# Two heads side by side in the values products, dilated scores in head pairs, and a hint ahead of the overflow branch

## The chip, the cores and the metric

The kernel runs on one core of a Trainium2 chip, in one launch. The time is device microseconds of one execution; the number to be told is the median of several runs. The engines are TensorE (PE in the profile; PEld are its weight loads), VectorE (DVE), ScalarE (ACT), GpSimd (POOL) and SyncE (SP, which issues most DMAs).

## The reference

Two blocks of two layers each work on 256 tokens of width 1024, all in fp32. A layer of the first block has a mixer of global attention (8 query heads, 2 key heads) and dilated attention (12 heads in three groups of 4, summed by their log-sum-exp weights), and then 16 experts with two chosen per token. A layer of the second block has four branches, among them neighbourhood attention and attention on a memory (4 heads each), and a feed-forward net. Cut to the attention, which the change touches:

```python
def _global_gqa(q, k, v):                       # 8 heads of 64
    sc = jnp.einsum('bqgrd,bkgd->bgrqk', qi, k).astype(jnp.float32) * scale
    p = jax.nn.softmax(sc, axis=-1)
    return jnp.einsum('bgrqk,bkgd->bqgrd', p.astype(v.dtype), v)

def _dilated_group(q, k, v, window, dilation, slopes):   # three groups of 4 heads
    sc = jnp.einsum('bqhd,bqkhd->bhqk', qi, kg).astype(jnp.float32) * scale + bias[None, :, None, :]
    sc = jnp.where(valid[None, None], sc, -jnp.inf)
    lse = jax.nn.logsumexp(sc, axis=-1)
    p = jnp.exp(sc - lse[..., None])
    o = jnp.einsum('bhqk,bqkhd->bqhd', p.astype(v.dtype), vg)
    return o, lse.transpose(0, 2, 1)
# in _mixer: the three groups of one head are one softmax over all their keys
    wts = jax.nn.softmax(jnp.stack(lses, 0), axis=0)
    out_b = jnp.sum(wts[..., None].astype(h.dtype) * jnp.stack(outs, 0), 0).reshape(b, s, B_OUT)

def memory_attention(q, mk, mv):                # neighbourhood attention is alike, with a bias
    sc = jnp.einsum('bhsd,bhmd->bhsm', q, mk).astype(jnp.float32) * (q.shape[-1] ** -0.5)
    p = jax.nn.softmax(sc, axis=-1)
    return jnp.einsum('bhsm,bhmd->bhsd', p.astype(mv.dtype), mv)
```

## The kernel before

Weights come in blocks of 128x2048 fp32 through SP's queue into four buffers (`wraw`). Each block is split into a high part by ScalarE (`whi`, L60) and a low part by VectorE (`wlo`, L66), and a product with weights is three matmuls of such parts (`mm3`, L251 to L253). Attention itself works in plain fp32.

Tokens lie in two tiles of 128. `scores` and `exps` (L376, L379) take the maximum on VectorE and the exponent on ScalarE, which also sums it into `zz`. `values` then transposes the probabilities on PE (L1045, in `full_attn` L1545), ScalarE copies them out of PSUM into `pt`, and PE multiplies with the probabilities as the stationary operand and 64 columns of values as the moving one (L1052, L1551): tokens come out on the partitions. After all heads `heads_out` (L386, L391) multiplies by the reciprocal of the sums and transposes back, and `split_to` (L398, L399) makes a high and a low part for the next product.

The dilated attention goes over 4 heads and 2 token tiles. Each step makes three scores products of 256 columns, one for each of the three groups (L1088), with 64 rows of the array since a head has 64 features, adds the bias on VectorE (L1089), and after the exponent has 6 transposes (L1100), two copies (L1102) and 6 values products (L1107).

Between these steps stand jobs that need only PE and weights: `fill` takes one from a list (projections and gates, 48 matmuls of 256 columns each), `tick` takes a piece of the conditioning (`ada_acc`, L456, on VectorE). The instructions of GpSimd and SP stand as written; those of PE, VectorE and ScalarE are ordered by the Tile scheduler, except where the program turns that off (`manual_schedule`).

In the experts `moe` reads a flag after the fourth: if a group has over 128 tokens, `moe_rest` (fp32 products for the rest) runs, else it is jumped over (L1330). With the tokens of this case it is jumped over in both layers. On PE `moe_rest` is 4 groups of 80 matmuls and transposes: 16 to gather, 2 transposes, 2 for the weights, 4 experts of 14, and 4 to scatter.

Of the kernel before, what the change touches and what calls it, by code (L numbers as in the profile page):

```python
# [8 lines left out]
F = mybir.dt.float32  # L9
# [3 lines left out]
OP = mybir.AluOpType  # L13
AX = mybir.AxisListType

DEPTH = 2
# [7 lines left out]
SLOPES = [2.0 ** (-8.0 * (h + 1) / 12) for h in range(12)]  # L24
TU = ((0, 2, 3, 6), (2, 3, 4, 6))
# [10 lines left out]
NB8, NRAW, NHL, NT2, NZ1 = 9, 4, 6, 6, 4  # L36
# [136 lines left out]
class Net:  # L173
# [205 lines left out]
            nc.scalar.activation(p[:, i], s[:, i], AF.Exp, bias=nm[:, i:i + 1], accum_out=zz[i])  # L379
        return p  # L380

    def heads_out(self, o, rz, nh, t, hi, lo):

        nc = self.nc
        n = self.t2([128, nh, 64], name="on")
        nc.vector.tensor_mul(n, o.rearrange("p (h d) -> p h d", d=64), rz[:, :, None].to_broadcast([128, nh, 64]))  # L386
        nf = n.rearrange("p h d -> p (h d)")
        p = self.tp()
        m = nh // 2
        for f in range(m):  # L390
            nc.tensor.transpose(p[:, f * 128:(f + 1) * 128], nf[:, f * 128:(f + 1) * 128], self.ident)  # L391
        ts = slice(t * 128, (t + 1) * 128)
        self.split_to(hi[:, :, ts], lo[:, :, ts], p[:, :m * 128].rearrange("p (f w) -> p f w", f=m))

    def split_to(self, hi, lo, ps, scale=None):
        nc = self.nc
# [543 lines left out]
    def mixer(self, l, hT):  # L940
        nc, a = self.nc, self.a
        w = a["win"][l]
# [69 lines left out]
        for jj in range(2):  # L1012
            p = self.tp()
# [12 lines left out]
        ob = [self.acc("oacc") for _ in range(2)]  # L1026

        def scores(j):
            pr = []
# [8 lines left out]
            return pr  # L1038

        def values(j, pr):  # L1040
            for h in range(2):
                p = self.tp()
                for t in range(2):
                    for c in range(2):
                        nc.tensor.transpose(p[:, c * 256 + t * 128:c * 256 + (t + 1) * 128],  # L1045
                                            pr[h][:, t, c * 128:(c + 1) * 128], self.ident)
                pt = self.t2([128, 2, 256], name="pt")
                nc.scalar.copy(pt, p.rearrange("p (c q) -> p c q", c=2))
                n = 2 * j + h
                for t in range(2):  # L1050
                    for c in range(2):
                        nc.tensor.matmul(ob[t][:, n * 64:(n + 1) * 64], pt[:, c, t * 128:(t + 1) * 128],  # L1052
                                         va[:, c, h * 64:(h + 1) * 64], start=(c == 0), stop=(c == 1))
        self.bg_on = True
        for j in range(4):
            pr = scores(j)
# [4 lines left out]
                self.tick()  # L1061
            self.fill()
            values(j, pr)
        rz = self.small([128, 2, 8], "att_rz", 2)
        nc.vector.reciprocal(rz, zz)
        for t in range(2):
            self.heads_out(ob[t], rz[:, t], 8, t, oa[:, 0], oa[:, 1])
        if l == DEPTH - 1:
            self.decay_log(0)

# [6 lines left out]
        od = [self.acc("obacc") for _ in range(2)]  # L1077
        for j in range(4):
            hs = slice(j % 2 * 64, (j % 2 + 1) * 64)
            for t in range(2):  # L1080
                sb = self.sm.tile([128, 3, 256], F, name="sbias", tag="z1", bufs=NZ1)
                s = self.sb()
                for g in range(3):
                    if g == 2:
                        s = self.sb()
                    sv = s[:, (g % 2) * 256:(g % 2 + 1) * 256]
                    ch = 2 * g + j // 2
                    nc.tensor.matmul(sv, qdT[hs, ch, t * 128:(t + 1) * 128], kdT[hs, ch, :], start=True, stop=True)  # L1088
                    nc.vector.scalar_tensor_tensor(sb[:, g], dist[t][g], -SLOPES[4 * g + j], sv,  # L1089
                                                   op0=OP.mult, op1=OP.add)  # L1090
                self.exps(sb.rearrange("p g w -> p (g w)")[:, None, :], [zz[:, t, j:j + 1]], 1, 768, True)
                if (2 * j + t) in TU[l]:
                    self.tick()
                self.fill()
                pt = self.sm.tile([128, 3, 256], F, name="ptd", tag="z1", bufs=NZ1)
                for g0, n in ((0, 2), (2, 1)):
                    p = self.tp()
                    for g in range(g0, g0 + n):
                        for c in range(2):
                            nc.tensor.transpose(p[:, (2 * (g - g0) + c) * 128:(2 * (g - g0) + c + 1) * 128],  # L1100
                                                sb[:, g, c * 128:(c + 1) * 128], self.ident)
                    nc.scalar.copy(pt[:, g0:g0 + n], p[:, :n * 256].rearrange("p (g w) -> p g w", g=n))  # L1102
                for g in range(3):
                    h = 4 * g + j
                    for c in range(2):
                        v = vd0[:, c, h * 64:(h + 1) * 64] if h < 8 else vd1[:, c, (h - 8) * 64:(h - 7) * 64]
                        nc.tensor.matmul(od[t][:, j * 64:(j + 1) * 64], pt[:, g, c * 128:(c + 1) * 128], v,  # L1107
                                         start=(g == 0 and c == 0), stop=(g == 2 and c == 1))
        rz = self.small([128, 2, 8], "att_rz", 2)
        nc.vector.reciprocal(rz[:, :, :4], zz[:, :, :4])  # L1110
        for t in range(2):
            self.heads_out(od[t][:, :256], rz[:, t, :4], 4, t, ob[:, 0], ob[:, 1])
        mr = self.b8([128, 8, 256], name="mr")
        for b in range(2):
            hl = self.wblk(a["wa"][l, b], 4)
# [164 lines left out]
    def moe(self, l, st, sc2, sh2, g2):  # L1280
# [21 lines left out]
        for e in range(NE + 1):  # L1302
# [36 lines left out]
    def moe_y(self, y, g2):  # L1339

        yy = self.b8([128, 2, 1024], R, name="yy")
        vs = []
        for hf in range(2):
            hs = slice(hf * 512, (hf + 1) * 512)
            v = self.t2([128, 512], name="yg")
            self.nc.vector.tensor_mul(v, y[hf], g2[:, hs])
            vs.append(v)
        for hf in range(2):
            hs = slice(hf * 512, (hf + 1) * 512)
            self.split_to(yy[:, 0, hs], yy[:, 1, hs], vs[hf])  # L1350
        return yy

    def moe_rest(self, l, pos, z, sc2, sh2, cw, xb, g2):

# [164 lines left out]
    def full_attn(self, qT, kT, v, voff, bias, oh, ol):  # L1519
# [4 lines left out]
        for hp in range(2):  # L1524
            pr = []
            for i in range(2):
# [11 lines left out]
                pr.append(self.exps(sv, [zz[:, t, h:h + 1] for t in range(2)], inplace=bias is not None))  # L1538
            self.fill()
            for i in range(2):  # L1540
                h = 2 * hp + i
                p = self.tp()
                for t in range(2):
                    for c in range(2):
                        nc.tensor.transpose(p[:, c * 256 + t * 128:c * 256 + (t + 1) * 128],  # L1545
                                            pr[i][:, t, c * 128:(c + 1) * 128], self.ident)
                pt = self.t2([128, 2, 256], name="pt")
                nc.scalar.copy(pt, p.rearrange("p (c q) -> p c q", c=2))  # L1548
                for t in range(2):
                    for c in range(2):  # L1550
                        nc.tensor.matmul(o[:, t * 256 + h * 64:t * 256 + (h + 1) * 64],  # L1551
                                         pt[:, c, t * 128:(t + 1) * 128], v[:, c, voff + h * 64:voff + (h + 1) * 64],
                                         start=(c == 0), stop=(c == 1))
        rz = self.small([128, 2, 8], "att_rz", 2)
        nc.vector.reciprocal(rz[:, :, :4], zz[:, :, :4])
        for t in range(2):
            self.heads_out(o[:, t * 256:(t + 1) * 256], rz[:, t, :4], 4, t, oh, ol)

    def block2(self, l):
        nc, a = self.nc, self.a  # L1560
# [369 lines left out]
```

## Time and profile before

| what | value |
|---|---|
| median of 3 runs | 1786.83 us (1784.20 to 1789.61) |
| profiled execution | 1785.33 us, span 1783.5 us |
| PE busy | 1705.8 us (96%) |
| VectorE busy | 1203.2 us (67%) |
| ScalarE busy | 890.8 us (50%) |
| GpSimd busy | 152.2 us (9%) |
| mean granted clock of PE | 0.974 |
| moved by DMA | 374.16 MB |

The span goes from the first to the last instruction of the program on the chip; some 2 us of the execution lie around it. Busy times of PE are of overlapping matmuls, so that a matmul's price is the distance to the start of the next one. An fp32 matmul is two rows in the trace, one made of `mm3` parts is one row. First-layer attention lies at 80 to 234 us, second-layer at 524 to 682, the experts at 290 to 490 and 740 to 935, the attention of the second block at 1048 to 1094 and 1476 to 1522.

### The profile page before, as it was taken

Reading aid. Unit: us, or ns where it says so; the run is one execution under the profiler, and the core shown is the slowest. Engines: PE = TensorE matmul, PEld = TensorE weight load, DVE = VectorE, ACT = ScalarE, POOL = GpSimd, SP = SyncE. Lnnn points to the kernel's source line nnn. Section 1 sums busy time; section 2 is a strip of 40 time slices with the busy share of each in tenths; the row PEclk is TensorE's granted clock in tenths of the full one; section 3 lists DMA queues with packets and bytes.
Section 4 is the critical chain, followed back from the end, with each engine's and each line's share of the span. In section 5 each row is a group of like instructions: output and inputs, shape, how many; then the busy total and the mean of one; then the engine's idle time right before and its main releaser. Section 6 shows DMA issues by size and latency. Waiting matters only on the chain. (4 is left out here: it accounts for less than half of the span.)

```text
span 1783.5 us, 26246 instructions
## 1 busy us (share of the span) xinstructions
PE 1705.8 (96%) x10666; PEld 1502.2 (84%) x10666; DVE 1203.2 (67%) x1565; ACT 890.8 (50%) x1268; POOL 152.2 (9%) x187
## 2 busy tenths in 40 slices
PE   6899999879999999998999999999999999999999
PEld 6798897768788889776777899999987889989997
DVE  7868778859987746886997465665545555575553
ACT  1544446747654344675765354454444445454442
POOL 3100011110020001101011210000001020000000
PEclk9889999989999999988999999999999999999999
DMA  8768752869757735277976353455555453445552
GB/s 317 273 242 320 255 193 71 301 249 349 274 200 262 269 138 196 76 271 289 337 283 229 124 193 133 172 178 189 185 193 194 165 194 132 164 148 195 183 186 71
DMA packets 56338, 374.16 MB, mean 210 GB/s; under 512 B 6896, under 2 KB 7056, under 8 KB 14224
## 3 DMA queue, kind: packets, MB, share of 16 engines
q1 hardware_dynamic: 50256, 352.41, 55.4%
q0 software_dynamic: 5952, 19.97, 3.2%
q8 instruction: 88, 1.44, 0.3%
q14 instruction: 42, 0.34, 0.1%
HBM read 370.25 MB, written 2.10 MB: 209 GB/s over the span
## 5 line engine op out<-in xcount | busy, mean ns | idle before, releaser
L66 DVE TENSOR_TENSOR wlo<-wraw,whi 128x1024 fp32r<-128x1024 f32 x562 | 676.5, 1225 | 335.2 <-ACT whi L60 327.7
L60 ACT CAST whi<-wraw 128x1024 fp32r<-128x1024 f32 x572 | 588.5, 1050 | 450.5 <-PE acc L252 230.2
L251 PE MATMUL acc<-fm_hi,whi 128*128 128x256 f32 x1536 | 442.3, 288 | 0.0
L252 PE MATMUL acc<-fm_lo,whi 128*128 128x256 f32 x1536 | 439.8, 286 | 0.0
L253 PE MATMUL acc<-fm_hi,wlo 128*128 128x256 f32 x1536 | 438.1, 285 | 0.0
L251 PEld LDWEIGHTS acc<-fm_hi,whi 128*128 128x128 f32 x1536 | 297.2, 193 | 10.6 <-issue 9.2
L252 PEld LDWEIGHTS acc<-fm_lo,whi 128*128 128x128 f32 x1536 | 297.5, 194 | 3.1 <-issue 3.0
L253 PEld LDWEIGHTS acc<-fm_hi,wlo 128*128 128x128 f32 x1536 | 297.2, 194 | 1.9 <-issue 1.9
L262 POOL TENSOR_TENSOR rs_r<-rs_v,mhalf 128x1 f32<-128x1 f32 (+3 forms) x52 | 56.8, 1093 | 993.7 <-DVE rs_v L261 986.5
L251 PE MATMUL acc<-whi,fm_hi 128*128 128x512 f32 (+1 forms) x384 | 137.6, 360 | 3.1 <-ACT fm_hi L323 3.1
L253 PE MATMUL acc<-whi,fm_lo 128*128 128x512 f32 (+1 forms) x384 | 135.1, 352 | 4.2 <-DVE fm_lo L324 4.1
L252 PE MATMUL acc<-wlo,fm_hi 128*128 128x512 f32 (+1 forms) x384 | 135.6, 353 | 1.6 <-DVE wlo L66 1.6
L251 PE MATMUL gu<-whi,hgh 128*128 128x512 f32 x256 | 107.5, 420 | 12.3 <-PEq L1330 10.0
L252 PE MATMUL gu<-wlo,hgh 128*128 128x512 f32 x256 | 105.5, 412 | 3.5 <-issue 2.0
L253 PE MATMUL gu<-whi,hgl 128*128 128x512 f32 x256 | 104.2, 407 | 0.0
L456 DVE SCALAR_TENSOR_TENSOR ada_acc<-wraw,cond,ada_acc 128x1024 f32<-128x1024 f32 x74 | 94.6, 1279 | 1.4 <-DMA wraw<-in_ada 0.4
L253 PEld LDWEIGHTS acc<-whi,fm_lo 128*128 128x128 f32 x384 | 74.2, 193 | 14.3 <-DVE fm_lo L324 5.7
L252 PEld LDWEIGHTS acc<-wlo,fm_hi 128*128 128x128 f32 x384 | 74.2, 193 | 13.2 <-DVE wlo L66 4.7
L251 PEld LDWEIGHTS acc<-whi,fm_hi 128*128 128x128 f32 x384 | 73.9, 193 | 13.1 <-ACT fm_hi L323 4.1
L251 PEld LDWEIGHTS gu<-whi,hgh 128*128 128x128 f32 x256 | 50.8, 199 | 25.1 <-PEq L1330 11.1
L252 PE MATMUL acc<-wlo,act_hi 128*128 128x512 f32 x176 | 68.6, 390 | 0.0
L251 PE MATMUL acc<-whi,act_hi 128*128 128x512 f32 x176 | 68.6, 390 | 0.0
(391 smaller groups left out, 2695.8 us busy)
## 6 DMA issues: line engine op xcount, KB each, us to landing
wraw<-in_moe SPq DMA_DIRECT2D x96, 1024.0 KB, 5.0
wraw<-in_win SPq DMA_DIRECT2D x58, 1024.0 KB, 4.9
wraw<-in_ffi SPq DMA_DIRECT2D x44, 1024.0 KB, 4.8
wraw<-in_ada SPq DMA_DIRECT2D x40, 1024.0 KB, 5.3
wraw<-in_wg SPq DMA_DIRECT2D x32, 1024.0 KB, 4.8
wraw<-in_ffo SPq DMA_DIRECT2D x22, 1024.0 KB, 4.8
wraw<-in_wo SPq DMA_DIRECT2D x16, 1024.0 KB, 4.8
wraw<-in_ada SPq DMA_DIRECT2D x16, 512.0 KB, 8.0
```

The source lines that it names most:

```text
L60: net.nc.scalar.copy(h, self.r[:, i * 1024:(i + 1) * 1024])
L66: (eng or net.nc.vector).tensor_sub(l, self.r[:, i * 1024:(i + 1) * 1024], h.bitcast(F))
L251: mm(ps, l[0], r[0], start=first, stop=False)
L252: mm(ps, l[0], r[1], start=False, stop=False)
L253: mm(ps, l[1], r[0], start=False, stop=last)
L262: nc.gpsimd.tensor_tensor(r[:, :n], v[:, :n], self.mhalf[:, :n], op=OP.pow)
L456: nc.vector.scalar_tensor_tensor(acc, rv, self.cond[:, f:f + 1], acc, op0=OP.mult, op1=OP.add)
```

## The change

Three things are changed.

1. The values products of all four kinds of attention. VectorE multiplies the probabilities by the reciprocal of their sum before they are transposed (`share`); the transposes and the copy are now in `p_fm`; in `two_heads` the 64 columns of values are stationary, the transposed probabilities are moving (256 tokens, in the dilated attention 128), and the two heads of a pair write partitions 0 to 63 and 64 to 127 of one PSUM tile, taking turns. Features come out on the partitions, so `heads_out` is gone, and `split_to` follows each pair.
2. The dilated attention goes over 2 head pairs and 2 token tiles: for each group the scores of the two heads follow each other, each into its own PSUM bank; then exponents, reciprocals and scaling of both, transposes of both, and 12 values products.
3. A branch hint for PE is placed: for the first layer's `moe_rest` at the start of the program, for the second layer's in the else branch of the first. The condition itself is unchanged.

```diff
-    def heads_out(self, o, rz, nh, t, hi, lo):
...
-        nc.vector.tensor_mul(n, o.rearrange("p (h d) -> p h d", d=64), rz[:, :, None].to_broadcast([128, nh, 64]))
...
+    def share(self, p, rz):
+
+        for i in range(p.shape[1]):
+            self.nc.vector.tensor_scalar_mul(p[:, i], p[:, i], rz[:, i:i + 1])
+
+    def p_fm(self, p):
+
+        q = self.tp()
+        for t in range(2):
+            for c in range(2):
+                self.nc.tensor.transpose(q[:, c * 256 + t * 128:c * 256 + (t + 1) * 128],
+                                         p[:, t, c * 128:(c + 1) * 128], self.ident)
+        pt = self.t2([128, 2, 256], name="pt")
+        self.nc.scalar.copy(pt, q.rearrange("p (c q) -> p c q", c=2))
+        return pt
+
+    def two_heads(self, o, pts, vs):
+
+
+        n = len(pts[0])
+        for c in range(n):
+            for i in range(2):
+                self.nc.tensor.matmul(o[i * 64:(i + 1) * 64], vs[i][c], pts[i][c], start=(c == 0), stop=(c == n - 1))
...
         def values(j, pr):
+            rz = self.small([128, 2, 2], "att_rz", 2)
+            nc.vector.reciprocal(rz, zz[:, :, 2 * j:2 * j + 2])
+            pts = []
             for h in range(2):
...
+                self.share(pr[h], rz[:, :, h])
+                pts.append(self.p_fm(pr[h]))
+            if j % 2 == 0:
+                bank["o"] = self.acc("oacc")
+            o = bank["o"][:, j % 2 * 256:(j % 2 + 1) * 256]
+            self.two_heads(o, [[pt[:, c] for c in range(2)] for pt in pts],
+                           [[va[:, c, h * 64:(h + 1) * 64] for c in range(2)] for h in range(2)])
+            self.split_to(oa[:, 0, j], oa[:, 1, j], o)
...
+        od = self.acc("obacc")
+        for jp in range(2):
             for t in range(2):
...
+                for gs in ((0, 1), (2,)):
+                    ss = [self.sb() for _ in range(2)]
+                    for g in gs:
+                        for i in range(2):
+                            hs = slice(i * 64, (i + 1) * 64)
+                            nc.tensor.matmul(ss[i][:, g % 2 * 256:(g % 2 + 1) * 256],
+                                             qdT[hs, 2 * g + jp, t * 128:(t + 1) * 128], kdT[hs, 2 * g + jp, :],
+                                             start=True, stop=True)
...
+                    self.exps(sv, [zz[:, t, 2 * jp + i:2 * jp + i + 1]], 1, 768, True)
...
+                    nc.vector.reciprocal(rz[:, i:i + 1], zz[:, t, 2 * jp + i:2 * jp + i + 1])
+                    self.share(sv, rz[:, i:i + 1])
...
+                self.two_heads(od[:, jp * 256 + t * 128:jp * 256 + (t + 1) * 128],
+                               [[pt[:, g, c * 128:(c + 1) * 128] for g in range(3) for c in range(2)] for pt in pts], vs)
+            self.split_to(ob[:, 0, jp], ob[:, 1, jp], od[:, jp * 256:(jp + 1) * 256])
...
-                with self.tc.If(flag > 0):
+                with self.tc.If(flag > 0, label=f"rest{l}") as more:
                     self.moe_rest(l, pos, z, sc2, sh2, cw, xb, g2)
+                with more.Else():
+                    if l + 1 < DEPTH:
+                        self.hint_rest(l + 1)
...
+    def hint_rest(self, l):
+
+        self.tc.mark_branch_hint_location(f"rest{l}", "LikelyTaken", engines=[mybir.EngineType.PE])
...
+            pts = [self.p_fm(pr[i]) for i in range(2)]
+            ops = o[:, hp * 256:(hp + 1) * 256]
+            vo = voff + 128 * hp
+            self.two_heads(ops, [[pt[:, c] for c in range(2)] for pt in pts],
+                           [[v[:, c, vo + i * 64:vo + (i + 1) * 64] for c in range(2)] for i in range(2)])
+            self.split_to(oh[:, hp], ol[:, hp], ops)
...
+        self.hint_rest(0)
```

Three places show how the order of PE's instructions moves. The first is the dilated attention of the first layer, one head and one token tile before (`sbias` are the probabilities, `dil` queries, keys and values, `obacc` the outputs; `acc` belongs to a gate job):

```order
L1100 MATMUL tp<-ident,sbias 128x128 x6
L1088 MATMUL sb<-dil 128x256 x2
L1107 MATMUL obacc<-dil,ptd 128x64 x6
L1088 MATMUL sb<-dil 128x256
L489 MATMUL tp<-ada_acc,ones 128x512 x2
```

The same place now, for a pair of heads and one token tile:

```order
L1116 MATMUL tp<-ident,sbias 128x128 x6
L1092 MATMUL sb<-dil 128x256 x2
L1116 MATMUL tp<-ident,sbias 128x128 x6
L404 MATMUL obacc<-ptd,dil 64x128
L1092 MATMUL sb<-dil 128x256
L404 MATMUL obacc<-ptd,dil 64x128 x11
L1092 MATMUL sb<-dil 128x256 x2
```

The transposes of two heads stand around the next pair's first scores; a sixth scores product follows 10 gate matmuls later; in between are twelve values products where there were twice six.

The second place is PE at the neighbourhood attention of the second block's first layer (`sx` are the probabilities, `nkT` and `nqT` keys and queries, `bun` the values, `oat` the outputs), before:

```order
L1545 MATMUL tp<-ident,sx 128x128 x8
L1531 MATMUL sb<-nkT,nqT 128x256 x3
L1551 MATMUL oat<-bun,pt 128x64 x8
L1531 MATMUL sb<-nkT,nqT 128x256
```

and now:

```order
L392 MATMUL tp<-ident,sx 128x128 x8
L1554 MATMUL sb<-nkT,nqT 128x256 x3
L404 MATMUL oat<-pt,bun 64x256 x4
L1554 MATMUL sb<-nkT,nqT 128x256
```

Four products of 256 columns stand where eight of 64 columns stood; the neighbours are the same.

The third place is PE at the end of the first layer's `moe_rest`, before (`rest_hy` and `rest_d` belong to moe_rest, `gu` to the fifth expert after the branch):

```order
L1407 MATMUL tp<-rest_hy,rest_d 128x512 x4
L1330 UNCONDITIONAL_BRANCH x2
L251 MATMUL gu<-whi,hgh 128x512
L252 MATMUL gu<-wlo,hgh 128x512
```

and now:

```order
L1430 MATMUL tp<-rest_hy,rest_d 128x512 x4
L1346 UNCONDITIONAL_BRANCH
L1942 BRANCH_PREFETCH_HINT
L1346 UNCONDITIONAL_BRANCH
L251 MATMUL gu<-whi,hgh 128x512
L252 MATMUL gu<-wlo,hgh 128x512
```

The hint for the second layer's branch stands where the first one jumps to; the other hint is PE's second instruction of the program.

## Rows read from the trace of the kernel before

**Rows 1.** The page's busy times: us, share of the span, instructions of each engine.

```profile
PE 1705.8 (96%) x10666; PEld 1502.2 (84%) x10666; DVE 1203.2 (67%) x1565; ACT 890.8 (50%) x1268; POOL 152.2 (9%) x187
```

**Rows 2.** Windows: stretch, length; busy us of PE, PEld, DVE, ACT, POOL; clock, DMA, GB/s.

```profile
132.00:234.00 102.00, 101.97 (x720) 90.44 (x719) 80.04 (x92) 47.06 (x75) 1.08 (x2) 1.00 0.79 279
362.00:379.00 17.00, 9.66 (x25) 6.85 (x24) 2.51 (x3) 1.92 (x2) 1.13 (x2) 0.60 0.50 182
379.00:480.00 101.00, 100.95 (x440) 79.61 (x439) 89.86 (x98) 72.34 (x93) 0.00 (x0) 1.00 0.87 325
```

**Rows 3.** Timeline of PE, neighbourhood attention: start, length in us, instruction, count, idle before.

```profile
1486.06 2.00 PE L1551 MATMUL oat<-bun,pt 128*128 128x64 f32 x16
1487.99 0.70 PE L1531 MATMUL sb<-nkT,nqT 64*128 64x256 f32 x2
```

**Rows 4.** Timeline of PE at the pooling branch, a product of 64 stationary columns.

```profile
970.86 1.09 PE L1664 MATMUL sb<-band,bun 128*64 128x256 f32 x8
971.88 0.39 PE L253 MATMUL acc<-fm_hi,wlo 128*128 128x256 f32 x1
972.10 0.28 PE L251 MATMUL acc<-fm_hi,whi 128*128 128x256 f32 x1
972.22 0.28 PE L252 MATMUL acc<-fm_lo,whi 128*128 128x256 f32 x1
```

**Rows 5.** Timeline of PE: dilated attention, and scores of the neighbourhood attention.

```profile
155.66 1.13 PE L1088 MATMUL sb<-dil 64*128 64x256 f32 x4
156.72 1.55 PE L1107 MATMUL obacc<-dil,ptd 128*128 128x64 f32 x12
158.20 0.70 PE L1088 MATMUL sb<-dil 64*128 64x256 f32 x2
158.83 1.13 PE L489 MATMUL tp<-ada_acc,ones 128*128 128x512 f32 x2
...
1476.92 1.14 PE L1531 MATMUL sb<-nkT,nqT 64*128 64x256 f32 x8
```

**Rows 6.** Timeline of PE at the transposes of the first layer's global attention.

```profile
131.60 1.04 PE L391 MATMUL tp<-ident,on 128*128 128x128 f32 x8
132.39 0.47 PE L251 MATMUL acc<-whi,fm_hi 128*128 128x512 f32 x1
```

**Rows 7.** Line 1330, the branch: engine, operation, count, ns shortest/median/longest, first and last start.

```profile
L1330 ACTq COMPARE_BRANCH  x2: 45/48/50, 361.3 to 810.9; - x2
L1330 PEldq COMPARE_BRANCH  x2: 5560/5596/5632, 362.1 to 811.7; - x2
```

**Rows 8.** DMA queues from 362 to 376 us: packets, MB, share of 16 engines.

```profile
q8 instruction: 3, 0.05, 1.5%
```

**Rows 9.** Timeline of PE at the two branches; in brackets idle before, and its releaser.

```profile
361.44 1.20 PE L1298 MATMUL acc<-yy,dT 128*128 128x512 f32 x4 [0.65 <-DVE yy L399]
367.95 0.76 PE L251 MATMUL gu<-whi,hgh 128*128 128x512 f32 x1 [5.32 <-PEq L1330]
...
372.01 0.80 PE L252 MATMUL gu<-wlo,hgh 128*128 128x512 f32 x1 [2.01 <-issue]
...
378.15 0.43 PE L251 MATMUL gu<-whi,hgh 128*128 128x512 f32 x1
...
811.23 1.71 PE L1298 MATMUL acc<-yy,dT 128*128 128x512 f32 x4 [0.67 <-DVE yy L399]
817.62 0.77 PE L251 MATMUL gu<-whi,hgh 128*128 128x512 f32 x1 [4.68 <-PEq L1330]
...
822.00 0.40 PE L252 MATMUL gu<-wlo,hgh 128*128 128x512 f32 x1
```

**Rows 10.** Groups by line on VectorE: operation, shapes, count | busy us, mean ns | idle before.

```profile
L454 DVE TENSOR_SCALAR ada_acc<-wraw,cond 128x1024 f32<-128x1024 f32 x6 | 4.5, 749 | 0.0
...
L1496 DVE TENSOR_SCALAR dexp<-steps,dec_l 128x512 f32<-128x512 f32 x8 | 3.5, 481 | 0.0
```

**Rows 11.** Waits of PE: who waited, for whom: us in total, times, longest us.

```profile
PE tp L1045 <- ACT prob L379: 3.1, 1, 3.1
```

More of the change, by code (lines that the diff above doesn't have):

```diff
@@ L380, in exps @@
         return p
-    def heads_out(self, o, rz, nh, t, hi, lo):
-        nc = self.nc
-        n = self.t2([128, nh, 64], name="on")
-        nc.vector.tensor_mul(n, o.rearrange("p (h d) -> p h d", d=64), rz[:, :, None].to_broadcast([128, nh, 64]))
[L387 to L393, printed above, removed]
+    def share(self, p, rz):
[15 more added lines that the diff above has]
+                self.nc.tensor.matmul(o[i * 64:(i + 1) * 64], vs[i][c], pts[i][c], start=(c == 0), stop=(c == n - 1))
     def split_to(self, hi, lo, ps, scale=None):
@@ L1025, in mixer @@
         zz = self.small([128, 2, 8], "att_z", 2)
-        ob = [self.acc("oacc") for _ in range(2)]
         def scores(j):
@@ L1040, in values @@
         def values(j, pr):
+            rz = self.small([128, 2, 2], "att_rz", 2)
+            nc.vector.reciprocal(rz, zz[:, :, 2 * j:2 * j + 2])
+            pts = []
             for h in range(2):
[L1042 to L1053, printed above, removed]
+                self.share(pr[h], rz[:, :, h])
[6 more added lines that the diff above has]
+            self.split_to(oa[:, 0, j], oa[:, 1, j], o)
+        bank = {}
         self.bg_on = True
@@ L1063, in mixer @@
             values(j, pr)
[L1064 to L1067, printed above, removed]
         if l == DEPTH - 1:
@@ L1076, in mixer @@
         zz = self.small([128, 2, 8], "att_z", 2)
-        od = [self.acc("obacc") for _ in range(2)]
-        for j in range(4):
-            hs = slice(j % 2 * 64, (j % 2 + 1) * 64)
+        od = self.acc("obacc")
+        for jp in range(2):
             for t in range(2):
[L1081 to L1112, printed above, removed]
+                sb = [self.sm.tile([128, 3, 256], F, name="sbias", tag="z1", bufs=NZ1) for _ in range(2)]
+                for gs in ((0, 1), (2,)):
[6 more added lines that the diff above has]
+                                             start=True, stop=True)
+                    for g in gs:
+                        for i in range(2):
+                            nc.vector.scalar_tensor_tensor(sb[i][:, g], dist[t][g], -SLOPES[4 * g + 2 * jp + i],
+                                                           ss[i][:, g % 2 * 256:(g % 2 + 1) * 256],
+                                                           op0=OP.mult, op1=OP.add)
@@ new lines, in mixer @@
+                rz = self.small([128, 2], "att_rz", 2)
+                pts = []
+                for i in range(2):
+                    sv = sb[i].rearrange("p g w -> p (g w)")[:, None, :]
+                    self.exps(sv, [zz[:, t, 2 * jp + i:2 * jp + i + 1]], 1, 768, True)
+                    if 2 * (2 * jp + t) + i in TU[l]:
+                        self.tick()
+                    self.fill()
+                    nc.vector.reciprocal(rz[:, i:i + 1], zz[:, t, 2 * jp + i:2 * jp + i + 1])
+                    self.share(sv, rz[:, i:i + 1])
@@ new lines, in mixer @@
+                for i in range(2):
+                    pt = self.sm.tile([128, 3, 256], F, name="ptd", tag="z1", bufs=NZ1)
+                    for g0, n in ((0, 2), (2, 1)):
+                        p = self.tp()
+                        for g in range(g0, g0 + n):
+                            for c in range(2):
+                                nc.tensor.transpose(p[:, (2 * (g - g0) + c) * 128:(2 * (g - g0) + c + 1) * 128],
+                                                    sb[i][:, g, c * 128:(c + 1) * 128], self.ident)
+                        nc.scalar.copy(pt[:, g0:g0 + n], p[:, :n * 256].rearrange("p (g w) -> p g w", g=n))
+                    pts.append(pt)
@@ new lines, in mixer @@
+                vs = [[], []]
+                for i in range(2):
+                    for g in range(3):
+                        h = 4 * g + 2 * jp + i
+                        vs[i] += [vd0[:, c, h * 64:(h + 1) * 64] if h < 8 else vd1[:, c, (h - 8) * 64:(h - 7) * 64]
+                                  for c in range(2)]
+                self.two_heads(od[:, jp * 256 + t * 128:jp * 256 + (t + 1) * 128],
+                               [[pt[:, g, c * 128:(c + 1) * 128] for g in range(3) for c in range(2)] for pt in pts], vs)
@@ L1538, in full_attn @@
                 pr.append(self.exps(sv, [zz[:, t, h:h + 1] for t in range(2)], inplace=bias is not None))
+            rz = self.small([128, 2, 2], "att_rz", 2)
+            nc.vector.reciprocal(rz, zz[:, :, 2 * hp:2 * hp + 2])
+            for i in range(2):
+                self.share(pr[i], rz[:, :, i])
             self.fill()
[L1540 to L1557, printed above, removed]
+            pts = [self.p_fm(pr[i]) for i in range(2)]
[4 more added lines that the diff above has]
+            self.split_to(oh[:, hp], ol[:, hp], ops)
     def block2(self, l):
```

## Prediction

> **What bounds the kernel now.** The page's busy line comes first: TensorE (PE) shows 1705.8 of 1783.5 us, VectorE 67%, ScalarE 50% [rows 1]. A busy PE is not yet a PE that sets the time, so the stages come next. In the dilated attention of the first layer (132 to 234 us) PE has 101.97 busy of 102.00, beside 80.04 of VectorE and a DMA share of 0.79; in the experts (379 to 480) it has 100.95 of 101.00, beside 89.86 and 0.87. Only around the branch (362 to 379) is it 9.66 of 17.00, at a granted clock of 0.60 [rows 2]. So PE's instructions in order, with their stalls, are the time, and what leaves PE's queue shortens it unless an engine that feeds it becomes late. I then read the distances from start to start on PE around each step that the change touches, since shown durations of matmuls overlap.
>
> **Values products of global, neighbourhood and memory attention.** An fp32 matmul is two rows in the trace. Before, a head pair has 8 matmuls of 128x64 with the probabilities stationary: 16 rows from 1486.06 until the next instruction at 1487.99, 1.93 us [rows 3]. After, it has 4 matmuls of 64 stationary columns and 256 moving ones, the two heads writing the two halves of the partitions. The pooling branch of the kernel already has exactly that shape: 8 rows from 970.86 until 971.88, 1.02 us, and 0.1 more behind (971.88 to 972.10 is 0.22, the next step 0.12) [rows 4]. That halves run side by side is seen there: these 8 rows last 1.09 us, while four unpaired rows of as many moving columns, in the dilated scores, last 1.13 [rows 5]. The gain is 0.91 a pair; I take 0.9. There are 4 pairs in the global attention and 4 in the two calls of full_attn, in two layers each: 16 x 0.9 = 14.4 us.
>
> Of that 0.1, the Trainium skill, TensorEngine Tiling (Array Packing), Key Properties, says something that goes further: changing the tiling mode drains TensorE. If each change cost the emptying of a matmul, 0.28 us as shown at 972.10 instead of 0.1, two changes for each of 24 head groups would bring the sum out 8.6 us later, an estimate. The rows do not show it.
>
> **Dilated scores and values.** Before, one head and token tile has on PE 4 rows of scores, 12 of values and 2 of scores, from 155.66 to 158.83, 3.17 us; two heads take 6.3 [rows 5]. After, a pair of heads has six scores matmuls of two row halves; the order on PE, shown ahead, puts them as 2, 1, 2 and 1. A pair of row halves runs side by side in a row of before too: 8 rows of the neighbourhood scores last 1.14 us, as 4 of the dilated ones do [rows 5]. So a block of two is as long as a block of one, 0.63 (158.20 to 158.83), and four are 2.5. The values are 24 rows of 64 stationary and 128 moving columns, 12 for each half. A step of a pair at 256 columns is 1.02 / 4, some 0.22 without the switch; half the columns give 0.11, so 12 steps are 1.3; the one product that stands apart, and five or six changes at 0.1, add 0.8. The sum is 4.6, against 6.3: 1.7 a group, and eight groups (2 pairs x 2 tiles x 2 layers) give 13.6 us. The other end: did the 24 rows run one after another at 0.11, they would take 2.7, and the gain would be some 0.5 a group, 4 us.
>
> **Transposes of the outputs.** The new products come out with features on the partitions, so the 40 transposes in heads_out go. Eight of them take from 131.60 to 132.39, 0.79 [rows 6]; the runs of two elsewhere pay more of the 0.1 changes. At 0.1 to 0.15 each, 5 us.
>
> **The branch.** On PE the jump over moe_rest lasts 5.56 and 5.63 us, on ScalarE 0.05 [rows 7]. What differs is how much code lies between: on PE moe_rest is 4 groups of 80 matmuls and transposes. The queue that carries instructions moves three packets, 0.05 MB, between 362 and 376 [rows 8], and soon after the jump PE stops again for 2.01 us with "issue" as the reason [rows 9]. So it waits for code. PE idles 5.32 + 2.01 and 4.68 us, and runs at half clock until about 378.15 and 822.00: 10.20 us from 367.95 for 19 matmuls (8.2 without the stall), and 4.38 from 817.62 for 10 [rows 9]. At the 0.23 a matmul of the stage behind (100.95 us for 440, [rows 2]) they are 4.4 and 2.3, so 3.8 and 2.1 more are lost. Together 17.9 us. I keep 15: the flag is still waited for (0.4 each time), and the combining matmuls ahead of the second branch are already slow, 1.71 us for four at 811.23 against 1.20 at 361.44 [rows 9], so the second loss of clock stays in part. What the hint does is in no row of before. Its bounds are no gain (one instruction more) and 17.9; and below nothing, if it fetched the wrong code, another stall like the 2.01 at each branch, 4. I take the upper part because the distance is what costs here, not the decision, and both hints stand on PE long ahead of their branch.
>
> **What is added.** VectorE now scales probabilities. Multiplying 128x512 by a column takes 0.48 us, 128x1024 takes 0.75 [rows 10]; on that line 256 columns are 0.35 and 768 are 0.61. With 64 of the first, 16 of the second, 24 more reciprocals and without heads_out's products, about 30 us of VectorE are added. Spread over 1203 busy us there is room, but they lie in a chain: exponent, reciprocal, scaling, transposes, copy, product. The first pair already waits 3.1 us for the exponent [rows 11]; the new product needs the copies of both heads, and the dilated transposes of two heads now follow each other through two banks. Fill matmuls cover most of it; I put 0.3 us on each of 24 groups, 7.2 us, between nothing and 0.6. Queued behind a reciprocal that waits for ScalarE is VectorE's next weight split (wlo), for which PE's next block waits. In the first dilated stage VectorE goes from 80 to some 85 us of about 95, and I put 3 us on that.
>
> **Sum.** 14.4 + 13.6 + 5 + 15 - 7.2 - 3 = 37.8 us off the profiled execution's 1785.3 (the span of 1783.5 and 1.8 around it): 1747.5. That execution is 1.5 us under the median of the three runs, so the forecast is 1749.
>
> **The rivals.** *The hint does nothing* (0.21): the 15 us are not gained, 22.8 are, and the time is 1764. For it speaks that the first hint stands some 360 us ahead of its branch, and that no row shows such a thing at work. *Column halves do not run side by side* (0.08): the first term is nothing and the second 4, so 13.8 are gained, 1773. Against it are the 8 rows of the pooling product [rows 4]. The Trainium skill, TensorE: Matmul & The Clock Gate, Part 3, says that weight loads overlap running matmuls only when the row groups differ, and column halves share theirs; by that rule this rival would hold, and the trace so far does not agree. *Both* (0.06): 1.2 lost, 1788, which is no change. *The chain turns into a wait* (0.07): if each of 24 groups held PE for the first pair's 3.1 us, 74 us would stand against the 48 gained, 1813. It decides from 2.0 us a group (48 / 24). Against it speaks that most groups have 48 matmuls of fill, near 6 us at 0.12, beside a chain of about 5 (the 3.1, two scalings and a copy); for it, that VectorE and PE both work in order.
>
> **How the numbers follow.** The forecast of 1749 has 0.58. Its own error is the waits (7 either way), the branch (3 less) and the dilated groups and their VectorE (5 either way), so 1734 to 1761, and 1732 at the outside. The first rival at 1764 lies inside a range up to 1774, with half of the second; left out are the last two, half of the second and the forecast's own edges, under 0.2. A measurement of this kernel can tell about 0.3%, 5.4 us, from no change. Faster by more than that: 0.87; within it: 0.06; slower: 0.07.
>
> **What would show it.** In the changed kernel: values products of 8 rows in about 1.0 us and of 24 in about 1.4; PE's branch under 0.6 us, with no stall and no low clock behind the first one; no transposes of "on"; PE waiting less than 10 us in all for scaled probabilities and copies. Eight values rows that take 1.8 us would make the second rival true, a branch still of 5 us the first. VectorE idle on ScalarE with wlo behind it, and PE's clock falling inside the attention stages, would make the prediction wrong.

## The result, and the profile after

The changed kernel takes 1744.06 us (median of 4 runs, 1739.57 to 1746.34), beside 1786.74 for the kernel before on the same chip: ratio 0.9758, 95% interval 0.9733 to 0.9783, faster by 43 us. The forecast was 1749, with a range of 1732 to 1774.

The profiled execution has a span of 1743.1 us, 40.4 less than before. PE is still the engine that is busy 96% of the time, now with 168 rows of matmuls less; VectorE gained 16.5 us of work, where the forecast had added up about 30. The page's busy times, beside [rows 1]:

```profile
PE 1667.9 (96%) x10498; PEld 1451.3 (83%) x10498; DVE 1219.7 (70%) x1657; ACT 890.6 (51%) x1272; POOL 155.0 (9%) x187
```

The windows that answer to [rows 2] (same columns): the first dilated attention, the stretch of the branch, the experts behind it. The stretch of the branch has 10.70 of 11.00 us busy and a granted clock of 0.84, where it had 9.66 of 17.00 and 0.60; the experts are as they were, 440 matmuls in 101 us.

```profile
130.00:230.00 100.00, 99.53 (x779) 88.27 (x778) 79.55 (x105) 48.62 (x77) 1.76 (x3) 1.00 0.72 267
351.00:362.00 11.00, 10.70 (x40) 8.21 (x40) 4.50 (x6) 4.26 (x5) 1.13 (x2) 0.84 0.91 289
362.00:463.00 101.00, 100.95 (x440) 79.55 (x439) 91.36 (x103) 71.01 (x90) 0.57 (x1) 1.00 0.90 333
```

**The branch.** Line 1346 is the branch that was 1330. Its group (columns as in [rows 7]), and PE's timeline there, beside [rows 9]: PE spends 0.35 and 0.40 us on the jump, waits 0.30 us each time, and "issue" is gone.

```profile
L1346 PEldq COMPARE_BRANCH  x2: 350/376/403, 351.4 to 781.3; - x2
```

```profile
350.78 1.63 PE L1314 MATMUL acc<-yy,dT 128*128 128x512 f32 x4 [0.64 <-DVE yy L410]
352.71 0.77 PE L251 MATMUL gu<-whi,hgh 128*128 128x512 f32 x1 [0.30 <-PEq L1346]
...
354.88 0.40 PE L253 MATMUL gu<-whi,hgl 128*128 128x512 f32 x1
...
782.80 0.77 PE L251 MATMUL gu<-whi,hgh 128*128 128x512 f32 x1 [0.30 <-PEq L1346]
```

Matmuls of 0.63 us, the length at the lower clock, end at about 354.9, 2.2 us after the first matmul behind the branch; in [rows 9] they lasted from 367.95 to 378.15.

**The products of a pair.** Two timelines of PE answer to [rows 3]; line 404 is the product in `two_heads`. The pair at 123.21 takes 1.01 us to the next start, as forecast. The pair at 1446.98 takes 1.49. Read pair by pair along PE's timeline, ten of the 16 are of that kind, four have their first product alone with a background matmul behind it, one takes 1.23, and one, that at 123.21, is what was forecast. Counted from start to start without what stands between, the products of all 16 pairs go from 31.9 us before to 25.8.

```profile
123.21 1.08 PE L404 MATMUL oacc<-pt,va 128*64 128x256 f32 x8
124.22 0.50 PE L253 MATMUL acc<-whi,fm_lo 128*128 128x512 f32 x1
```

```profile
1446.98 1.56 PE L404 MATMUL oat<-pt,bun 128*64 128x256 f32 x8
1448.47 0.70 PE L1554 MATMUL sb<-nkT,nqT 64*128 64x256 f32 x2
```

The timeline of ScalarE at that pair tells why. Its two copies, one for each head, last 1.07 us together: the first is over at about 1446.9, where PE begins, the second at 1447.4. The first head's first product starts alone, and by the start times in the trace so does the last one: only the four rows between start two by two, some 7 ns apart, where at 123.21 all eight do.

```profile
1446.34 1.07 ACT L395 COPY pt<-tp 128x512 f32<-128x512 f32 x2
```

**A group of the dilated attention**, beside [rows 5]: PE's timeline in the first layer (1092 scores, 1116 transposes, 404 products).

```profile
156.60 0.70 PE L1092 MATMUL sb<-dil 64*128 64x256 f32 x4
157.23 0.88 PE L1116 MATMUL tp<-ident,sbias 128*128 128x128 f32 x6
158.04 0.43 PE L404 MATMUL obacc<-ptd,dil 128*64 128x128 f32 x2
158.40 0.70 PE L1092 MATMUL sb<-dil 64*128 64x256 f32 x2
159.02 1.52 PE L404 MATMUL obacc<-ptd,dil 128*64 128x128 f32 x22
160.48 0.70 PE L1092 MATMUL sb<-dil 64*128 64x256 f32 x4
161.11 0.39 PE L251 MATMUL acc<-fm_hi,whi 128*128 128x256 f32 x1
```

The products take 0.36 + 1.46 us, two heads for which [rows 5] have 1.48 each. Two scores of two halves take 0.63 (160.48 to 161.11), and one alone takes 0.62 (158.40 to 159.02): what stands alone costs as much as a pair. Both the first product and the scores behind it stand alone here. The first product does so in all eight groups, with lone scores behind it in six and background matmuls in two.

### The profile page after: what moved, and what is told of

The parts are those of the page before. It is cut to its first block, busy times and chain, and to the rows that moved or that the text cites. A ratio compares the mean times of both kernels' runs of the same rounds, so it can differ in the third digit from the quotient of the medians.

```text
span 1743.1 us, 26009 instructions
## 1 busy us (share of the span) xinstructions
PE 1667.9 (96%) x10498; PEld 1451.3 (83%) x10498; DVE 1219.7 (70%) x1657; ACT 890.6 (51%) x1272; POOL 155.0 (9%) x187
## 5 line engine op out<-in xcount | busy, mean ns | idle before, releaser
L252 PEld LDWEIGHTS acc<-wlo,fm_hi 128*128 128x128 f32 x384 | 74.5, 194 | 13.6 <-DVE wlo L66 4.9
L253 PE MATMUL acc<-whi,act_lo 128*128 128x512 f32 x176 | 68.5, 389 | 0.0
```

The source lines that it names most:

```text
L252: mm(ps, l[0], r[1], start=False, stop=False)
L253: mm(ps, l[1], r[0], start=False, stop=last)
```

## Experiments

Times are medians, and each ratio is to the kernel before on the same chip. From one set of runs to another the changed kernel moved by 1.6 us (1744.06 and 1745.63) and the kernel with the pairs' copies by chunk, below, by 4.8 (1738.47 and 1743.23), so that differences across sets are known to some us only. The attention alone, the dilated loop undone, the first exchange of the loops, the copy and the scaling are compared with the changed kernel across sets.

**The two halves of the change.** The hint alone, on the kernel before:

```
-                with self.tc.If(flag > 0):
+                with self.tc.If(flag > 0, label=f"rest{l}") as more:
...
+                with more.Else():
+                    if l + 1 < DEPTH:
+                        self.hint_rest(l + 1)
```

> The kernel before with nothing changed but the branch: label, else part and the two hint marks. Theory (the hint takes the instruction fetch out of the path and adds to the rest): 15 us less than before, 1771 to 1773 us, with COMPARE_BRANCH on TensorE's queues near 0.4 us instead of 5.6 us and the half-clock stretch behind it at 3.4 us instead of 13.7 and 10.2 us. Rival 1 (the hint works only because the attention of the changed kernel leaves the fetch time for it, or the gain seen at the branch is taken from work beside it): 1780 us or more. Rival 2 (the hint is worth more than I gave it, the attention less): under 1768 us.

Measured: 1769.38 us beside 1783.88 of before, ratio 0.9914 (0.9895 to 0.9932): 14.5 us. And the attention alone, the same diff backwards on the changed kernel:

> The changed kernel with the branch as before, the attention as changed. Theory (parts add up): 15 us more than the changed kernel, 1758 to 1760 us, and the two branches at 5.6 us each again. Rival (the stages of attention hold most of the 40 us and the branch little): 1750 us or less.

Measured: 1760.75 us, ratio 0.9860 (0.9837 to 0.9883): 23.1 us under before and 15 to 17 over the changed kernel. The branch in the first and in the second of these kernels:

```profile
L1330 PEldq COMPARE_BRANCH  x2: 350/372/393, 362.6 to 800.7; - x2
```

```profile
L1346 PEldq COMPARE_BRANCH  x2: 5288/5538/5787, 355.8 to 792.4; - x2
```

The two parts add up within some us (14.5 + 23.1 = 37.6, beside 40 to 43 for both), and neither lives on the other. The hint came and went together with its label and the else part that holds it; they were not parted.

**The dilated loop undone**, with the lines of before (one head at a time, `heads_out` behind it):

```
-        od = self.acc("obacc")
-        for jp in range(2):
+        od = [self.acc("obacc") for _ in range(2)]
+        for j in range(4):
...
+        for t in range(2):
+            self.heads_out(od[t][:, :256], rz[:, t, :4], 4, t, ob[:, 0], ob[:, 1])
```

> The changed kernel with the dilated loop of before (heads one at a time, values moving, division and transposes at its end), all else as changed. Theory (the dilated stages and their tail gave 10.6 us of the 40, the forecast said 13.6 + 2.5 less the waits): 1753 to 1757 us. Rival 1 (the pairs' longer chain eats the gain, and the stages got faster from what the shorter fills leave): 1748 us or less. Rival 2 (the full 13.6 us and more): over 1759 us.

Measured: 1754.72 us, ratio 0.9827 (0.9805 to 0.9850), clear of the changed kernel's 0.9733 to 0.9783 and 0.9753 to 0.9797, so the dilated part is worth 9 to 11 us by the medians, and the others (global attention and the two of the second block) some 12 to 14 of the 23.

**Do the halves run side by side?** The two loops of the products exchanged:

```
-        for c in range(n):
-            for i in range(2):
+        for i in range(2):
+            for c in range(n):
                 self.nc.tensor.matmul(o[i * 64:(i + 1) * 64], vs[i][c], pts[i][c], ...
```

> The changed kernel with the two loops of the products of a pair exchanged: all chunks of the first head, then all of the second. The same products in the same column halves, but next to each other stand products of one half, which cannot run at the same time. Theory (halves side by side are where the gain of the values comes from): a dilated group's twelve products go from 1.25 us to about 2.5 us, 8 groups, 10 us; a pair of 256 columns from 1.49 or 1.02 us to about 1.7 us, 16 pairs, 3 to 6 us; 1756 to 1761 us. Rival (products of two halves follow each other anyway and the gain comes from fewer weight loads, the longer moving side and the transposes dropped): within 2 us of the changed kernel, 1742 to 1746 us.

Measured: 1742.76 us, ratio 0.9759 (0.9736 to 0.9783): no slower at all, and my theory seemed to have fallen. The timeline of PE says otherwise:

```profile
157.87 0.70 PE L1092 MATMUL sb<-dil 64*128 64x256 f32 x4
158.50 0.88 PE L1116 MATMUL tp<-ident,sbias 128*128 128x128 f32 x6
159.30 2.46 PE L404 MATMUL obacc<-ptd,dil 128*64 128x128 f32 x24
161.69 0.70 PE L1092 MATMUL sb<-dil 64*128 64x256 f32 x4
```

The 24 rows do take 2.39 us, not 1.82. But they stand in one row, and the lone scores product of 0.62 between them is gone: the scores keep to pairs. The exchange undid two things that nearly cancel: over the eight groups, from start to start, the products take 4.5 us more than in the changed kernel (19.1 beside 14.5) and the scores 2.5 less (17.0 beside 19.5), and the products of the 16 pairs 0.9 less. That leaves about 1 us, less than the runs can tell. On PE the scheduler sets the order; in the changed kernel the first head's first product is ready before its partner, so it goes ahead alone, and a scores product of the next group fills the gap alone. To tell the two apart, the order had to be held first.

**Both heads' chunks in one copy.** In the 16 pairs first: the transposes ordered by chunk instead of by head.

```
-    def p_fm(self, p):
+    def p_chunk(self, ps, c):
         q = self.tp()
-        for t in range(2):
-            for c in range(2):
-                self.nc.tensor.transpose(q[:, c * 256 + t * 128: ...], p[:, t, ...], ...)
+        for i in range(2):
+            for t in range(2):
+                self.nc.tensor.transpose(q[:, i * 256 + t * 128: ...], ps[i][:, t, ...], ...)
```

> The changed kernel with one thing more in global attention and in the full attentions of block 2: the eight transposes of a pair are ordered by chunk and not by head, so that each copy from PSUM brings one chunk of both heads, and the two products of a chunk can start together. Same instructions, same sizes, same answer. Theory (a pair's products come out at 1.49 us and not 1.02 us since the second head's copy is still under way when the first head's product starts, so that two products run alone): 12 of the 16 pairs get 0.4 us shorter, 4 to 6 us in all, 1738 to 1740 us, and the rows of the products by 0.4 us each. Rival (the products of 1.49 us are slow for another reason, such as the mode change of the array or the weight loads of 64 columns): 1743 to 1745 us, the rows as they are.

Measured: 1738.47 us, ratio 0.9741 (0.9721 to 0.9761). The run beside the changed kernel:

> x7_chunk_by_chunk as it is, beside the changed kernel on the same chip. Theory (a pair's two products start together): 4 to 6 us below the changed kernel, 1738 to 1740 us. Rival (its 5.6 us were between chips): within 2 us of it.

> The changed kernel as it is, beside x9_dilated_by_chunk on the same chip, so that the two can be compared directly: 1742 to 1746 us. If it comes out under 1740 us, what x7_chunk_by_chunk showed is partly the chip.

Measured: 1743.23 us (ratio 0.9760, 0.9739 to 0.9782) beside 1745.63 (0.9775, 0.9753 to 0.9797), only 2.4 us less, under what I expected of it, and the intervals overlap. That the whole is faster is not shown by the times. That the pairs are is shown by the rows: 14 of the 16 now take 1.01 to 1.07, and all together 18.5 us where they took 25.8. Where the other 5 of these 7 us went is not shown. The pair that took 1.49:

```profile
1446.98 1.08 PE L404 MATMUL oat<-pt,bun 128*64 128x256 f32 x8
1447.99 0.70 PE L1553 MATMUL sb<-nkT,nqT 64*128 64x256 f32 x2
```

Then the same in the dilated loop, on top of it:

```
-                for i in range(2):
-                    pt = self.sm.tile([128, 3, 256], F, name="ptd", ...)
-                    for g0, n in ((0, 2), (2, 1)):
+                for g in range(3):
+                    p = self.tp()
+                    for i in range(2):
                         for c in range(2): nc.tensor.transpose(...)
+                    pt = self.t2([128, 2, 256], name="ptd")
```

> The kernel of x7_chunk_by_chunk with the same done to the dilated loop: the twelve transposes of a group ordered by chunk, three banks with both heads in each, three copies of 512 columns and not four of 512 and 256. Same products, same answer. Theory (in the changed kernel the first head's first product of a group is ready before its partner, so the scheduler puts it ahead alone and a lone scores product behind it, which breaks a pair of products and a pair of scores in seven or eight groups of eight; that is where the exchange of loops in x3_head_after_head got back what it lost): the twelve products stand in a row as six pairs, 1.45 us and not 1.8 us, and fewer scores products stand alone at 0.63 us; 0.3 to 0.7 us in 8 groups, 2 to 5 us below x7_chunk_by_chunk, 1733 to 1736 us. Rival 1 (TensorE waits for the later transposes of both heads instead): 1738 us or more. Rival 2 (lone products and lone scores cost nothing, so x3 was even for another reason): 1737 to 1739 us with the rows shorter and the wait elsewhere.

Measured: 1734.43 us, ratio 0.9720 (0.9695 to 0.9744), 11.2 us under the changed kernel and 8.8 under the version before it on the same chip. A second run on another chip:

> x9_dilated_by_chunk as it is, beside x10_x9_head_after_head on the same chip: 1732 to 1737 us.

Measured: 1730.80 us, ratio 0.9692 (0.9677 to 0.9707). This version beats both kernels. In its timeline the products stand together and take 1.46 us:

```profile
158.39 1.53 PE L404 MATMUL obacc<-ptd,dil 128*64 128x128 f32 x24
159.85 1.13 PE L1091 MATMUL sb<-dil 64*128 64x256 f32 x6
```

Eight groups times 0.36 are 2.9 us. Most of the rest was waits behind the dilated stages, 5 us in the two layers. PE's longest wait from 150 to 250 us (columns as in [rows 11]) without the edit, where the stretch has 2.1 us of waits and none with it:

```profile
PE acc L251 <- ACT mrg_hi L1146: 1.3, 1, 1.3
```

PE's waits from 560 to 690 us without the edit, and with it, where this one line is all:

```profile
PE acc L251 <- DVE mr L1134: 1.1, 1, 1.1
PE tp L1115 <- ACT ptd L1117: 0.7, 2, 0.3
PE acc L251 <- ACT mrg_hi L1146: 0.5, 1, 0.5
PE acc L253 <- DVE mrg_lo L1147: 0.4, 1, 0.4
...
```

```profile
PE sb L1091 <- DVE sbias L1096: 0.2, 1, 0.2
```

I had expected 2 to 5 us of the edit, since I had counted the rows and not these waits.

**The halves again, in an order that holds.** The loops exchanged as above, now on this version:

> x9_dilated_by_chunk with the two loops of the products exchanged as in x3_head_after_head. Here the products of a group stand in one row either way and nearly all else on TensorE keeps its place, so that the order of the halves is the only thing that differs. Theory (halves side by side are worth what the rows say): a dilated group goes from 1.46 to 2.38 us as in x3, 8 groups, 7.4 us; a pair of 256 columns from about 1.05 to 1.4 to 1.5 us, 16 pairs, 6 to 7 us; 13 to 15 us above x9_dilated_by_chunk, 1747 to 1750 us. Rival (x3 was even because the products are hidden behind other work): within 3 us of x9_dilated_by_chunk.

Measured: 1747.18 us, ratio 0.9768 (0.9742 to 0.9795) beside 1730.80: 16.4 us slower. The row beside that of 158.39 above:

```profile
159.24 2.45 PE L404 MATMUL obacc<-ptd,dil 128*64 128x128 f32 x24
161.63 1.13 PE L1091 MATMUL sb<-dil 64*128 64x256 f32 x6
```

2.39 against 1.46 us, eight times, is 7.4; the products of the 16 pairs go from 18.5 to 25.0 us, 6.5 more, eight of them back at 1.50; the other 2.5 us are not placed. One of the eight:

```profile
1459.35 1.57 PE L404 MATMUL oat<-pt,bun 128*64 128x256 f32 x8 [0.20 <-ACT pt L395]
1460.84 0.48 PE L1552 MATMUL sb<-mkv,mqT 64*128 64x256 f32 x1
```

So the halves run side by side, and that is worth about 16 us where the order lets it.

**The second head's copy on VectorE:**

```
-        self.nc.scalar.copy(pt, q.rearrange(...))
+        if i: self.nc.vector.tensor_copy(pt, q.rearrange(...))
+        else: self.nc.scalar.copy(pt, q.rearrange(...))
```

> The changed kernel with the second head's copy from PSUM on VectorE and not on ScalarE, in global attention and the full attentions, so that the two copies of a pair run beside each other. Theory (ScalarE's two copies in a row are what holds the second head's products): the second copy ends about 0.2 us after the first and not 0.58 us, up to 0.4 us in 12 pairs, 2 to 5 us less, 1739 to 1742 us. Rival (VectorE takes its instructions in order and has other work ahead of the copy): 1744 us or more.

Measured: 1745.61 us, ratio 0.9787 (0.9760 to 0.9814): nothing gained. VectorE's timeline shows the copy behind two weight splits, and PE's that the first product now goes ahead alone here too, with lone scores behind it:

```profile
1444.19 2.35 DVE L66 TENSOR_TENSOR wlo<-wraw,whi 128x1024 fp32r<-128x1024 f32 x2
1446.47 0.68 DVE L396 COPY pt<-tp 128x512 f32<-128x512 f32 x1
```

```profile
1445.94 0.65 PE L407 MATMUL oat<-pt,bun 128*64 128x256 f32 x2
1446.51 0.70 PE L1557 MATMUL sb<-nkT,nqT 64*128 64x256 f32 x2
1447.20 1.08 PE L407 MATMUL oat<-pt,bun 128*64 128x256 f32 x6
```

**The price of the scaling.** This kernel leaves out the division of the softmax:

```
     def share(self, p, rz):
-        for i in range(p.shape[1]):
-            self.nc.vector.tensor_scalar_mul(p[:, i], p[:, i], rz[:, i:i + 1])
+        pass
```

> The changed kernel without the scaling of the probabilities by the reciprocal of their sum, ahead of the transposes: the division of the softmax is left out of all three attentions. Theory (the scaling stands on the chain from exponentials to transposes, and TensorE waits for it): 5 to 10 us less, 1734 to 1739 us, and the waits for VectorE's scaling at the transposes gone. Rival (background work covers it): within 2 us of the changed kernel.

Measured: 1749.12 us, ratio 0.9793 (0.9767 to 0.9819): 3 to 5 us above the changed kernel, whose intervals it overlaps, though VectorE lost 25 us of work. Both theories missed it. The profiled execution is the slowest of its four, and its mean granted clock was lower (0.975, beside 0.984 of the changed kernel), also in stretches that the edit hardly touches; the windows of the changed kernel and of this one there, the same stretch of time but not quite the same work:

```profile
945.00:1012.00 67.00, 64.44 (x441) 58.39 (x440) 37.58 (x71) 27.34 (x37) 16.92 (x16) 1.00 0.49 168
```

```profile
945.00:1012.00 67.00, 63.56 (x391) 55.10 (x390) 33.62 (x49) 26.67 (x37) 16.79 (x16) 0.95 0.47 161
```

That the clock made the difference is likely, not shown: its two runs at 0.980 and 0.982 take 1746.8 and 1746.7 us, and the changed kernel has 1743.2 to 1748.9 at these two. What the scaling costs stays open. PE's waits at the first pair of each layer, 7.6 us in the changed kernel, are 6.1 without it, but the waits for the merges behind the dilated stage (`mr`, `mrg_hi`) are all there, and longer:

```profile
PE acc L251 <- ACT mrg_hi L1146: 3.1, 2, 2.7
...
PE acc L251 <- DVE mr L1134: 1.7, 2, 1.4
```

## Why the prediction was right, point by point

**What bounds the kernel** held: 40.4 us came off the span, 37.9 off PE's busy time. Work taken from PE's queue was time.

**The branch**, 15 us, was the best-founded term: 14.5 alone, 15 to 17 beside the new attention. The first rival (0.21) is out. The row that carried it was the contrast of 5.6 us on PE and 0.05 on ScalarE [rows 7]. The Trainium skill, Runtime: NRT & Kernel Launch, Instruction fetch mechanics, says that a taken branch to a target outside the fetched window waits for a DMA; the trace agrees with 5.29 to 5.79 us without the hint and 0.35 to 0.40 with it. Of the instruction queue itself it shows little: from 345 to 385 us, the branch within, 4 packets before and 2 now.

**The dilated term** (13.6 and a fifth of the transposes, less 8 groups' waits and VectorE's 3) came to about 9; 9 to 11 were measured. On PE's rows, from start to start over all groups, scores and products went from 49.2 to 34.0 us, 15.2. Its step "the one product that stands apart" was seen in the order and priced nearly right, 2.1 us with the changes of mode against 1.82. What I did not ask is why it stands apart, and what it would be worth together: that was the 8.8 us of the last version.

**The values term was mis-sized.** Of 0.9 us a pair, the ten pairs of 1.49 give 0.44 (1.93 in [rows 3] less 1.49) and only one gives the whole; all 16 give 6.2 us (31.94 less 25.78) and not 14.4. The step that failed is the transfer from the pooling product [rows 4]: it has the shape, but both its operands lie ready, while here the second comes 0.5 us after the first. I did name the copies of both heads, as a wait that PE would see; it was a lost overlap inside a group of rows that looks busy.

**The waits were mis-sized the other way**, and hid part of it. I put 7.2 us on 24 groups. PE's waits in the changed kernel at the first pair of each layer:

```profile
PE sb L1044 <- ACT prob L379: 3.6, 1, 3.6
...
PE oacc L404 <- ACT pt L395: 2.6, 1, 2.6
```

With 1.4 us for the scaled probabilities of the second layer they are 7.6, but before had the 3.1 of [rows 11] and another 2.9 in the second layer:

```profile
PE oacc L1052 <- ACT pt L1048: 2.9, 1, 2.9
```

So these two places cost 1.6 us more, and the transposes of the second dilated stage 0.7. The 3 us for VectorE were right in size by luck: they came at another place, not in the dilated stage but behind it, where PE waits 1.3 (mrg_hi, 225 to 245 us) and 1.8 (mr, 660 to 680 us) for merges, as it did not before:

```profile
PE acc L251 <- ACT mrg_hi L1147: 1.3, 1, 1.3
...
PE acc L251 <- DVE mr L1135: 1.8, 1, 1.8
```

VectorE's added scaling is not their cause either: without it they are longer, and with the copies by chunk they are gone. The rival in which the chain turns into a wait is out, since these are single waits at few places and not 3.1 us on each of 24 groups.

**The rival on column halves** is refuted by 1.46 against 2.39 us for the same 24 rows. The Trainium skill, TensorE: Matmul & The Clock Gate, Part 3, has weight loads overlap only for different row groups; no such price is seen in these rows. The other rule weighed, the drain at a change of mode, would have made the sum 8.6 us worse; the rows show 0.1 us as before (behind the scores, 161.11 to 161.33 is 0.22, the step behind it 0.12).

**The sum** is closer than its terms. On PE's rows the values gave 6.2 us, the dilated part 14.7 (15.2 less 0.5 for the probabilities' transposes), the transposes of `heads_out` 3.4 and the two branches 15; other waits took 7 to 9, as the run goes. That is 30 to 33 of the 36 to 40 us by which the spans of two runs fell. The rest lies in rows that the change does not touch and that move from run to run: the products on `dd` around the experts take 27.5 us before, and 22.4 and 25.8 in two runs of the changed kernel. So that 1744 came so near to 1749 is in part luck. Of the signs named, the branch and the waits for probabilities and copies (8.9 us) came; the rows of 1.0 and 1.4 us did not, but for one pair, and some low clock behind the first branch stayed.

**The clock** rose by more than the branch explains. A mean over two levels that goes from 0.974 to 0.984 is some 37 us less at the lower one (0.026 x 2 x 1783.5 less 0.016 x 2 x 1743.1), and around the two branches it is some 17 (before, 17 us at 0.60 in [rows 2] and 17 at 0.70 from 808 us on; now 11 us at 0.84 and 14 at 0.88 from 778 us on). Another run of the changed kernel has 0.980, by which it is 23 us and not 37, and a span 4 us longer. How much of the rest the change owes, and how much is the run, stays open.

## What to carry to other kernels

When two products are to run side by side, ask not only for their shape but whether both operands become ready at once: let one copy bring the same chunk of both, and look in the order whether the scheduler keeps them together. A product that stands alone costs as much as a pair (0.62 beside 0.63 us here), and the engine still looks busy. An experiment that changes an order changes the scheduler's choices around it too; before calling a mechanism absent, hold the rest of the order still and repeat it.

## What the runs showed of the hardware

- Products of 64 stationary columns in two halves of the partitions take 1.46 us for 24 rows of 128 moving columns when the halves alternate, and 2.39 us when they follow each other by half, with the same products (the last version and its exchange).
- With the hint, PE's jump over some hundreds of instructions lasts 0.35 to 0.40 us, whether the attention ahead of it is the old or the new; without it 5.3 to 5.8.
- The same kernel differs by some us from run to run together with its mean clock: the exchange on the last version ran 1740.10 us at 0.986 and 1751.69 at 0.977. A single profile is no measure of a few us.
